# Same tile shapes in the RWKV chain, whole-width squares, and all PSUM banks in the last stage

## The chip, the core and the metric

The kernel runs on one core of one Trainium2 chip. The metric is the device time of one execution in microseconds (us). Before the change three runs took 1882.31, 1886.06 and 1886.7 us; the median is 1886.06.

## The reference, cut to what matters

One layer of a hybrid decoder for 1024 prompt tokens and 8 sample tokens that share all weights, in float32 (width 1024):

```python
h = rmsnorm(x, ln1); P = h @ w_in              # RWKV-7 | S5 | two merge gates
# RWKV-7, 8 heads of 64, for every token t:
sa = S @ (-kk_t)
S = S * w_t + outer(sa, kk_t * a_t) + outer(v_t, k_t)
y_t = S @ r_t                                  # then group norm, bonus, gate, w_rw_out
x += (sigmoid(g_rw) * rw + sigmoid(g_s5) * s5) @ w_out
x += ConvFFN(rmsnorm(x, ln2))                  # up 1024 -> 2 x 2816, causal conv, GELU gate, down
x += sigmoid(rmsnorm(x, ln3) @ w_ple_gate) * (p @ w_ple)
return rmsnorm(x, final_g), states
```

Each rmsnorm divides by the root of the mean square over the 1024 channels. Channels lie on partitions here (8 tiles of 128), so the sum over channels is a matmul with a matrix of ones over the tiles' summed squares.

## The kernel before, in words

Activations are stored transposed: 8 channel tiles of 128 partitions, tokens along the columns. Every float32 product with a large weight is split into two rounded parts ("hi" and "lo", fp32r), and each weight tile takes three matmuls, hi x hi, hi x lo and lo x hi. ScalarE (ACT) rounds the weight ("whi"), GpSimd (POOL) subtracts ("wlo"), and TensorE (PE) accumulates in a PSUM bank ("psm"). Plain float32 matmuls appear as two records each in the trace.

Stages: (1) the norm and the input projection in three blocks of 344 columns; (2) the S5 branch; (3) the RWKV recurrence, cut into chunks of 64 tokens, for 4 pairs of heads in two halves of 512 tokens, 8 units of 8 chunks; (4) the rest of the layer, in two "parts": columns 0 to 511 in one block of 512, and columns 512 to 1031 in two blocks of 260. Part 2 ends with the last stage (ple gate, final norm).

`chain` is the serial piece of stage 3. For chunk c with the state `So` it issues on PE: "S,AR" (`pp`, the state against the decayed keys, written to partitions 64 to 127), the two "Gm,UV" of the chunk before (`inner`, the part of the output inside a chunk, one per head, each to its half of the partitions), after a DVE addition (`pe`) the two "pe,Gm" (`up`, solving for the updates, one per head, to partitions 0 to 63), after a DVE copy (`UV`) "UV,BT" (`su`, the state's increment) and "AR,S" (the output from the old state). DVE then writes the new state `Sn`. The 64 x 64 heads make these matmuls differ in the rows and columns of the PE array that they use: a page row "128*64" is a matmul over 128 rows and 64 columns. Because other work is independent of the chain, projections ("psm") stand between its steps on PE.

The order on each engine is not written by hand. `Sched` records every operation with its dependencies and a priority, keeps an estimated cost per operation (and `SWITCH`, 90 ns, for a PE shape other than the one before), and repeatedly issues the operation that can start first on its modelled clock, by priority among those that could start then. A tile of a pool is handed out in the order in which the tiles of its tag were recorded. A change to one operation thus deals the order of all engines anew.

In `parts`, `sumsq` squares a tile on ACT into a buffer `sqt` (two of them, each claimed by a small memset on POOL) and adds it to `ssq`, on POOL for m up to 2 and on DVE above; `rstd` multiplies by ones on PE ("pstt"), and takes Ln and Exp on ACT into `rst`. In the last stage each tile m needs for each block a bank for the gate (`psg`) and one for `p @ w_ple` (`psp`). Part 2 has five banks of its own (`pm2`), while three (`pm`) of the eight are left from part 1. The last loop multiplies the 8 tiles by `rst`, tiles 3, 5 and 7 on POOL and the others on DVE, and stores them in pairs.

Of the kernel before, what the change touches and what calls it, by code (L numbers as in the profile page):

```python
# [9 lines left out]
F32 = mybir.dt.float32  # L10
F32R = mybir.dt.float32r
AF = mybir.ActivationFunctionType
# [5 lines left out]
P = 128  # L18
# [10 lines left out]
HW = 512  # L29
# [400 lines left out]
def build(tc, I, O, dbg=None):  # L430
# [106 lines left out]
    hs = ExitStack()  # L537
# [215 lines left out]

    def parts(ap, t0, n, blk, nmid, groups, pm, *nw):

# [57 lines left out]
        def sumsq(m, sl):  # L813
            if m == 0:
                G.tensor_tensor(ssq[:, sl], x2[m][:, sl], x2[m][:, sl], op=MUL)
            else:
                tmp = ta_("sqt", blk)
                S.activation(tmp, x2[m][:, sl], AF.Square)
                (V if m > 2 else G).tensor_tensor(ssq[:, sl], ssq[:, sl], tmp, op=ADD)

        def rstd(part=blocks):
            with g.prio(HI):
                for sl in part:
                    ps = pm.tile([P, blk], F32, name="pstt", tag="psm")
                    T.matmul(ps, ones, ssq[:, sl], start=True, stop=True)
                    S.activation(rst[:, sl], ps, AF.Ln, bias=epst[:, 0:1])
                sl = slice(part[0].start, part[-1].stop)
                S.activation(rst[:, sl], rst[:, sl], AF.Exp, scale=-0.5)
# [34 lines left out]
        with g.prio(HI):  # L863
            for m in range(8):
                hx.append(part(x2[m], "act", 8, pc("ln2", m)))
                with g.prio(HI + 1):
                    for sl in blocks:
                        sumsq(m, sl)

# [40 lines left out]
        with g.prio(HI):  # L910
            for k in range(2):
                pr = cv_()
                dma(pr, I["p"][k][:, tk])
                px.append(part(pr, "mid", nmid))
            for m in range(8):
                hx3.append(part(x2[m], "act", 8, pc("ln3", m)))
                with g.prio(HI + 1):
                    for sl in blocks:
                        sumsq(m, sl)
        for m in range(8):  # L920
            wg, wl = wtiles(I["w_ple_gate"][m], 8), wtiles(I["w_ple"][m], 2)
            pss = []
            for sl in blocks:
                with g.prio(MAIN):
                    psg = pm.tile([P, blk], F32, name="psm", tag="psm")
                    mmblk(psg, wg, hx3, sl.start, blk)
                    if m == 0 and len(blocks) == 1:
                        rstd()
                    psp = pm.tile([P, blk], F32, name="psm", tag="psm")
                    mmblk(psp, wl, px, sl.start, blk)  # L930
                    pss.append((psg, psp))
            if m == 0 and len(blocks) > 1:
                rstd()
            for sl, (psg, psp) in zip(blocks, pss):
# [8 lines left out]
        with g.prio(HI):  # L943
            if not shared:
                g.table("natural_log_exp_and_others", 6, rst[:, 0:1], tanh)
            for sl in blocks:
                rstd([sl])
                for m in range(8):
                    (G if m in (3, 5, 7) else V).tensor_tensor(x2[m][:, sl], x2[m][:, sl],
                                                               rst[:, sl], op=MUL)  # L950
                    if m % 2:
                        dma(O["y"][m - 1:m + 1, :, t0 + sl.start:t0 + sl.stop]
                            .rearrange("m p t -> p m t"), x2p[m // 2][:, :, sl])

    c2 = ExitStack()
    cvs = cp.tile([P, NH, 2], F32, name="cvs")
    parts(hp, 0, HW, HW, 4, (3, 2, 2, 3, 3, 3, 3, 3), pm, 2, 3)
    g.until_pools("rp", "p1", "pb", "pch", "py")
# [6 lines left out]
    parts(pool(c2, "pb_"), HW, NT - HW, (NT - HW) // 2, 5, (4, 3, 4, 4, 4, 3),  # L965
          pm2, 3, 5)
    g.drain()
# [308 lines left out]
def build_rwkv(g, rp, pb, pch, py, I, O, Pd, Wd, Ad, Yd, sg, ssh, omu, pc, pcs, dscr, dap, dma,  # L1276
# [35 lines left out]
    def headsum(ps, x, hi, bufs, lo):  # L1312
# [12 lines left out]
        T.matmul(ps, bor, lo, start=False, stop=True)  # L1325

    St = {}
    for k, j in ((0, 0), (1, 0), (2, 0), (3, 0), (0, 1), (1, 1)):
# [158 lines left out]
    def chain(p, hf, a, b):  # L1487
        AR, WC, Gm, BT, UV = a["AR"], a["WC"], b["Gm"], b["BT"], b["UV"]
        Y = py.tile([P, NC, CH], F32, name="Yps", tag="Y")
        ch = pch.tile([P, 3, P], F32, name="chp", tag="ch")  # L1490
        pp, up, su = ch[64:128, 0], ch[0:64, 1], ch[:, 2]
        heads = [slice(64 * h, 64 * h + 64) for h in range(2)]
# [8 lines left out]
        for c in range(NC):  # L1501
            n = hf * NC + c
            So, Sn = St[p, n % 2], St[p, (n + 1) % 2]
            first = n == 0

            if not first:
                T.matmul(pp, AR[:, c, 0], So, start=True, stop=True)
            if c:
                inner(c - 1, done, n == 1)
            pe = rp.tile([64, P], F32, name="pe", tag="pe", bufs=2)  # L1510
            gv = Gm[64:128, c, :, 0:64]
            if first:
                V.tensor_copy(pe.rearrange("p (h t) -> p h t", t=64), gv)
            else:
                h2 = lambda z: z.rearrange("p (h t) -> p h t", t=64)
                V.tensor_tensor(h2(pe), h2(pp), gv, op=ADD)
            for h, hs in enumerate(heads):
                T.matmul(up[:, hs], Gm[0:64, c, h, 0:64], pe[:, hs], start=h == 0, stop=h == 1)
            got = V.tensor_copy(UV[0:64, c], up)
# [227 lines left out]
```

## Time and profile before

| | us |
|---|---|
| median of three runs | 1886.06 |
| the profiled execution itself | 1882.29 |
| its span, first to last instruction | 1880.5 |
| PE busy in the span | 1815.4 |
| DVE busy | 1157.0 |
| ACT busy | 808.6 |
| POOL busy | 746.0 |

The span leaves out 1.8 us of the execution that lie around the first and the last instruction. A busy PE means that some matmul is in flight; matmuls overlap, so the distance between the starts of two of them, not a record's length, tells what one costs. The profile also gives the clock that was granted to PE, as a share of 2.4 GHz: 0.982 on average here.

### The profile page before, as it was taken

To read this page: it belongs to the slowest core of one execution; us is meant where nothing else is said; L and a number is where in the kernel's file an instruction comes from. 1 tells how busy PE (TensorE), PEld (TensorE's weight loads), DVE (VectorE), ACT (ScalarE), POOL (GpSimd) and SP (SyncE) were. 2 spreads that over 40 slices of the span, in tenths; PEclk is the share of its full clock that TensorE was granted. 3 is DMA by queue.
4 is the path that set the end of the run, shared out by engine and by line. 5 is a ranking of instruction groups with operands and counts; after the bars stand their busy time and mean duration, and the time that the engine had idled before them with its cause. 6 is when DMAs were issued, how large, how long until landed. Compare 5 with 4: busy or idle time off the path is not lost.

```text
span 1880.5 us, 32435 instructions
## 1 busy us (share of the span) xinstructions
PE 1815.4 (97%) x11946; PEld 1619.4 (86%) x11946; DVE 1157.0 (62%) x2386; ACT 808.6 (43%) x1455; POOL 746.0 (40%) x1089
## 2 busy tenths in 40 slices
PE   7999999999999999999999999999999999999987
PEld 6988888888889898986788888888889999999986
DVE  8899358767776786766555434446645444445565
ACT  4242444356543656444533333334554233333454
POOL 0000022124332433345555554455665444444453
PEclk9998999899999999999999999999999999999988
DMA  5534864323322254346343332233323233333322
GB/s 199 155 110 156 252 204 134 90 65 100 98 80 94 82 195 125 114 148 223 133 141 102 96 94 89 94 100 90 101 93 115 85 93 95 94 93 93 94 68 86
DMA packets 157950, 219.80 MB, mean 117 GB/s; under 512 B 48209, under 2 KB 81489, under 8 KB 157649
## 3 DMA queue, kind: packets, MB, share of 16 engines
q1 hardware_dynamic: 157792, 217.74, 36.9%
q8 instruction: 94, 1.54, 0.3%
q14 instruction: 64, 0.52, 0.1%
HBM read 174.94 MB, written 42.92 MB: 116 GB/s over the span
## 4 chain that ended last, share of the span: by engine, by line
PE 49%; DVE 4%; DMA 3%; POOL 2%; ACT 2%; issue 1%; SPq 0%; DVEq 0%; POOLq 0%; ACTq 0%
PE psm L417 47%; POOL wlo L417 1%; DVE x L417 1%; DVE cv L417 1%; PE chp L417 1%; DVE act L417 1%; DMA wraw<-in_w_out 1%; DMA wraw<-in_w_ffn_in 1%; DMA wraw<-in_w_ffn_out 0%; DMA wraw<-in_w_rw_out 0%; DMA wraw<-in_w_ple_gate 0%; ACT whi L417 0%; DMA gr<-gd 0%; DMA x<-in_x 0%; DVE mid L417 0%
## 5 line engine op out<-in xcount | busy, mean ns | idle before, releaser
L417 POOL TENSOR_TENSOR wlo<-wraw,whi 128x512 fp32r<-128x512 f32 (+2 forms) x432 | 550.4, 1281 | 475.2 <-ACT whi L417 428.5
L417 PE MATMUL psm<-act,whi 128*128 128x260 f32 (+1 forms) x2880 | 655.7, 322 | 3.9 <-ACT whi L417 2.2
L417 PEld LDWEIGHTS psm<-act,whi 128*128 128x128 f32 x2880 | 482.6, 189 | 53.3 <-ACT whi L417 4.1
L417 ACT ACTIVATE whi<-wraw 128x512 fp32r<-128x512 f32 (+2 forms) x468 | 275.0, 596 | 438.1 <-PE psm L417 269.4
L417 PE MATMUL psm<-act,wlo 128*128 128x260 f32 (+1 forms) x1440 | 461.8, 323 | 1.2 <-POOL wlo L417 1.1
L417 PE MATMUL psm<-mid,whi 128*128 128x260 f32 (+1 forms) x1344 | 307.5, 321 | 3.6 <-DVE cv L417 2.7
L417 PEld LDWEIGHTS psm<-act,wlo 128*128 128x128 f32 x1440 | 272.1, 189 | 26.6 <-POOL wlo L417 3.4
L417 PE MATMUL psm<-h1h,whi 128*128 128x344 f32 x816 | 273.6, 336 | 11.9 <-DVE h1h L417 11.9
L417 PE MATMUL psm<-h1l,whi 128*128 128x344 f32 x816 | 274.3, 336 | 0.1
L417 PE MATMUL psm<-h1h,wlo 128*128 128x344 f32 x816 | 271.8, 334 | 2.1 <-DVE wlo L417 2.1
L417 PEld LDWEIGHTS psm<-mid,whi 128*128 128x128 f32 x1344 | 222.8, 189 | 21.9 <-DVE cv L417 3.0
L417 PE MATMUL psm<-mid,wlo 128*128 128x260 f32 (+1 forms) x672 | 213.6, 322 | 0.2 <-POOL wlo L417 0.2
L417 PEld LDWEIGHTS psm<-h1h,whi 128*128 128x128 f32 x816 | 158.4, 194 | 16.4 <-issue 13.4
L417 DVE TENSOR_TENSOR x<-psm,x 128x260 f32<-128x260 f32 (+1 forms) x160 | 84.7, 531 | 133.8 <-PE psm L417 133.7
L417 PEld LDWEIGHTS psm<-h1h,wlo 128*128 128x128 f32 x816 | 158.5, 194 | 5.8 <-DVE wlo L417 2.4
L417 PEld LDWEIGHTS psm<-h1l,whi 128*128 128x128 f32 x816 | 158.5, 194 | 4.6 <-issue 1.1
L417 PEld LDWEIGHTS psm<-mid,wlo 128*128 128x128 f32 x672 | 126.7, 189 | 10.7 <-POOL wlo L417 0.6
L417 DVE TENSOR_TENSOR ta<-psm,rs 128x260 f32<-128x260 f32 (+1 forms) x66 | 34.0, 516 | 141.5 <-PE psm L417 132.9
L417 DVE SCALAR_TENSOR_TENSOR cv<-ta,par,cv 128x512 f32<-128x512 f32 x88 | 94.7, 1076 | 37.5 <-ACT cv L417 36.0
L417 DVE TENSOR_TENSOR mid<-cv,mid 128x260 fp32r<-128x260 f32 (+1 forms) x84 | 66.3, 795 | 26.4 <-ACT mid L417 25.6
L417 ACT ACTIVATE sw<-S,WC 64x64 f32<-64x64 f32 x120 | 41.1, 344 | 69.7 <-DVE S L417 67.8
L417 ACT ACTIVATE mid<-cv 128x260 fp32r<-128x260 f32 (+1 forms) x84 | 40.2, 487 | 59.4 <-DVE cv L417 54.0
(345 smaller groups left out, 2560.4 us busy)
## 6 DMA issues: line engine op xcount, KB each, us to landing
wraw<-in_w_ffn_in SPq DMA_DIRECT2D x176, 256.0 KB, 2.6
wraw<-in_w_in SPq DMA_DIRECT2D x68, 256.0 KB, 3.4
wraw<-in_w_ffn_out SPq DMA_DIRECT2D x64, 192.0 KB, 2.4
gd<-gt SPq DMA_DIRECT2D x16, 516.0 KB, 2.9
wraw<-in_w_out SPq DMA_DIRECT2D x32, 256.0 KB, 2.7
wraw<-in_w_ple_gate SPq DMA_DIRECT2D x32, 256.0 KB, 2.6
wraw<-in_w_ffn_out SPq DMA_DIRECT2D x32, 256.0 KB, 3.0
pd<-pt SPq DMA_DIRECT2D x12, 516.0 KB, 3.6
```

Of the source, the lines that this page charges most:

```text
L417: o.fn(*o.args, **o.kw)
```

## The change

1. In `chain`, "S,AR" takes both halves of `AR` as its weights and fills all 128 output partitions, of which the lower 64 are used. `pe` becomes one of two fixed tiles of 128 partitions, the upper 64 zeroed once, and "pe,Gm" contracts over all 128. The "Gm,UV" of the chunk before are recorded behind "pe,Gm" and wait for the DVE addition into `pe`, where they waited for the last chunk's state.
2. In `parts`, the squares for the second and third norm are taken over all columns of a part, in part 2 one of 520 where two of 260 were taken. (For the final norm they stay by block.)
3. `parts` is given a second pool of banks, `other`: for part 1 the same `pm`, for part 2 the three banks of part 1. In the last stage odd tiles use it for all but the first gate block, and the two "pstt" of the third norm lie in it.
4. The final norm of part 2 writes its factors twice: by one Exp to PSUM (`psr`), which DVE's products read, and by a second Exp to SBUF for POOL's.

```diff
-    def parts(ap, t0, n, blk, nmid, groups, pm, *nw):
+    def parts(ap, t0, n, blk, nmid, groups, pm, other, *nw):
...
-                tmp = ta_("sqt", blk)
+                tmp = ta_("sqt", sl.stop - sl.start)
...
-        def rstd(part=blocks):
+        def rstd(part=blocks, bank=None):
...
-                    ps = pm.tile([P, blk], F32, name="pstt", tag="psm")
+                    ps = (bank or pm).tile([P, blk], F32, name="pstt", tag="psm")
...
-                    for sl in blocks:
-                        sumsq(m, sl)
+                    sumsq(m, slice(0, n))
...
             pss = []
+            banks = [pm, other if m % 2 else pm]
             for sl in blocks:
+                if sl.start:
+                    banks[0] = banks[1]
                 with g.prio(MAIN):
-                    psg = pm.tile([P, blk], F32, name="psm", tag="psm")
+                    psg = banks[0].tile([P, blk], F32, name="psm", tag="psm")
...
-                    psp = pm.tile([P, blk], F32, name="psm", tag="psm")
+                    psp = banks[1].tile([P, blk], F32, name="psm", tag="psm")
...
-                rstd()
+                rstd(bank=other)
...
-                rstd([sl])
+                if shared:
+                    rstd([sl])
+                    rv = rst[:, sl]
+                else:
+                    ps = pm.tile([P, blk], F32, name="pstt", tag="psm")
+                    T.matmul(ps, ones, ssq[:, sl], start=True, stop=True)
+                    S.activation(rst[:, sl], ps, AF.Ln, bias=epst[:, 0:1])
+                    rv = other.tile([P, blk], F32, name="psr", tag="psm")
+                    S.activation(rv, rst[:, sl], AF.Exp, scale=-0.5)
+                    S.activation(rst[:, sl], rst[:, sl], AF.Exp, scale=-0.5)
                 for m in range(8):
-                    (G if m in (3, 5, 7) else V).tensor_tensor(x2[m][:, sl], x2[m][:, sl],
-                                                               rst[:, sl], op=MUL)
+                    if m in (3, 5, 7):
+                        G.tensor_tensor(x2[m][:, sl], x2[m][:, sl], rst[:, sl], op=MUL)
+                    else:
+                        V.tensor_tensor(x2[m][:, sl], x2[m][:, sl], rv, op=MUL)
...
+    rhs = []
+    for k in range(2):
+        t = rp.tile([P, P], F32, name=f"pe{k}")
+        G.memset(t[64:128], 0.0)
+        rhs.append(t)
...
-        pp, up, su = ch[64:128, 0], ch[0:64, 1], ch[:, 2]
+        pp, up, su = ch[:, 0], ch[0:64, 1], ch[:, 2]
...
             if not first:
-                T.matmul(pp, AR[:, c, 0], So, start=True, stop=True)
-            if c:
-                inner(c - 1, done, n == 1)
-            pe = rp.tile([64, P], F32, name="pe", tag="pe", bufs=2)
+                T.matmul(pp, AR[:, c].rearrange("p a b -> p (a b)"), So, start=True, stop=True)
+            pe = rhs[n % 2]
...
-                V.tensor_tensor(h2(pe), h2(pp), gv, op=ADD)
+                got = V.tensor_tensor(h2(pe[0:64]), h2(pp[0:64]), gv, op=ADD)
             for h, hs in enumerate(heads):
-                T.matmul(up[:, hs], Gm[0:64, c, h, 0:64], pe[:, hs], start=h == 0, stop=h == 1)
+                T.matmul(up[:, hs], Gm[:, c, h, 0:64], pe[:, hs], start=h == 0, stop=h == 1)
+            if c:
+                inner(c - 1, got, n == 1)
```

What this does to the order of the engines is shown at three places. First PE in the chain, one chunk between projections of 344 columns, before (a row gives output, operands and the output's size, "x2" that it stands twice):

```order
L417 MATMUL chp<-S_2733,AR 64x128
L417 MATMUL Yps<-Gm,UV 64x64 x2
L417 MATMUL psm<-h1h,whi 128x344
L417 MATMUL psm<-h1l,whi 128x344
L417 MATMUL psm<-h1h,wlo 128x344
L417 MATMUL chp<-pe,Gm 64x64 x2
...
L417 MATMUL chp<-UV,BT 128x128
L417 MATMUL Yps<-AR,S_2733 128x64
```

The same chunk of the changed kernel:

```order
L417 MATMUL chp<-S_2735,AR 128x128
L417 MATMUL psm<-h1h,whi 128x344
L417 MATMUL psm<-h1l,whi 128x344
L417 MATMUL psm<-h1h,wlo 128x344
...
L417 MATMUL chp<-pe_2730,Gm 64x64 x2
L417 MATMUL Yps<-Gm,UV 64x64 x2
...
L417 MATMUL chp<-UV,BT 128x128
L417 MATMUL Yps<-AR,S_2735 128x64
```

"S,AR" stands alone now and has the full size, and the two "Gm,UV" have moved behind the two "pe,Gm".

Second PE at the turn into the last stage, with buffer numbers, before: psm_11047 is the last bank of tile 0, psm_11061 the first of tile 1, the two pstt are the sums of the third norm.

```order
L417 MATMUL psm_11047<-mid_11012,wlo_11043 128x260
L417 MATMUL pstt_11048<-rs_10221,ones_66 128x260
L417 MATMUL pstt_11049<-rs_10221,ones_66 128x260
L417 MATMUL psm_11061<-act_11013,whi_11053 128x260 x2
L417 MATMUL psm_11061<-act_11013,wlo_11054 128x260
```

The same place now, where psm_11027 is the last bank of tile 0 and psm_11041 the first of tile 1:

```order
L417 MATMUL psm_11027<-mid_10999,wlo_11023 128x260
L417 MATMUL psm_11041<-act_11000,whi_11033 128x260 x2
L417 MATMUL psm_11041<-act_11000,wlo_11034 128x260
...
L417 MATMUL psm_11041<-act_11011,whi_11036 128x260 x2
L417 MATMUL pstt_11028<-rs_10215,ones_66 128x260
L417 MATMUL pstt_11029<-rs_10215,ones_66 128x260
L417 MATMUL psm_11041<-act_11011,wlo_11037 128x260
```

20 of the 24 matmuls of tile 1's first bank stand ahead of the two pstt now; none did.

Third POOL at the same place, from the split of tile 1's gate weights on, before (wlo is the split of a weight, 512 wide for a gate and 256 for the second product; sqt is the buffer of a square, tg one of the last stage):

```order
L417 TENSOR_TENSOR wlo<-wraw,whi 128x512 x2
L417 MEMSET sqt 128x2 x3
L417 TENSOR_TENSOR wlo<-wraw,whi 128x256
L417 MEMSET sqt 128x2 x2
L417 TENSOR_TENSOR wlo<-wraw,whi 128x512 x2
L417 MEMSET sqt 128x2 x3
L417 MEMSET tg 128x2 x2
```

And now:

```order
L417 TENSOR_TENSOR wlo<-wraw,whi 128x512 x2
L417 MEMSET sqt 128x2 x2
L417 TENSOR_TENSOR wlo<-wraw,whi 128x256
L417 MEMSET sqt 128x2
L417 TENSOR_TENSOR wlo<-wraw,whi 128x512
L417 MEMSET tg 128x2
```

Eight claims of a square's buffer stood there and three of them behind the splits of tile 2's gate weights; three stand there now, all ahead of those splits.

## Rows read from the trace of the kernel before

**Rows 1.** The page's totals: busy us, share of the span, instructions.

```profile
PE 1815.4 (97%) x11946; PEld 1619.4 (86%) x11946; DVE 1157.0 (62%) x2386; ACT 808.6 (43%) x1455; POOL 746.0 (40%) x1089
```

**Rows 2.** Stretches: length, busy us per engine, PE clock, DMA share, GB/s.

```profile
338.50:827.50 489.00, 480.26 (x3654) 418.19 (x3654) 356.85 (x950) 252.32 (x466) 165.50 (x289) 1.00 0.33 101
827.50:1018.40 190.90, 184.90 (x856) 148.06 (x854) 116.31 (x160) 81.12 (x148) 104.77 (x140) 0.98 0.50 166
1796.20:1812.50 16.30, 10.42 (x66) 8.33 (x65) 9.92 (x19) 8.94 (x20) 7.17 (x15) 0.85 0.25 81
1866.00:1880.50 14.50, 0.71 (x2) 0.30 (x2) 7.99 (x13) 3.49 (x7) 5.35 (x6) 0.60 0.43 147
...
1807.50:1817.80 10.30, 7.76 (x28) 6.29 (x29) 3.83 (x9) 6.42 (x11) 1.61 (x7) 0.50 0.12 42
```

**Rows 3.** Timeline of PE over one chunk: start, length, instruction, rows*columns, count.

```profile
570.90 0.32 PE L417 MATMUL psm<-h1l,whi 128*128 128x344 f32 x1
571.06 0.38 PE L417 MATMUL chp<-UV,BT 128*128 128x128 f32 x2
...
571.66 0.32 PE L417 MATMUL psm<-h1h,whi 128*128 128x344 f32 x1
...
572.14 0.32 PE L417 MATMUL psm<-h1h,whi 128*128 128x344 f32 x1
572.39 0.32 PE L417 MATMUL chp<-S,AR 128*64 128x128 f32 x1
...
573.13 0.32 PE L417 MATMUL psm<-h1h,wlo 128*128 128x344 f32 x1
573.29 0.32 PE L417 MATMUL psm<-h1h,whi 128*128 128x344 f32 x1
573.54 0.44 PE L417 MATMUL chp<-pe,Gm 64*64 64x64 f32 x4
...
574.17 0.32 PE L417 MATMUL psm<-h1h,wlo 128*128 128x344 f32 x1
...
574.96 0.32 PE L417 MATMUL psm<-h1l,whi 128*128 128x344 f32 x1
```

**Rows 4.** Timeline of PE where the two "Gm,UV" stand alone.

```profile
472.12 0.31 PE L417 MATMUL psm<-h1h,wlo 128*128 128x344 f32 x1
472.36 0.34 PE L417 MATMUL Yps<-Gm,UV 128*64 128x64 f32 x4
...
472.88 0.32 PE L417 MATMUL psm<-h1l,whi 128*128 128x344 f32 x1
```

**Rows 5.** Timeline of PE at the turn into the last stage.

```profile
1804.26 0.28 PE L417 MATMUL psm<-mid,wlo 128*128 128x260 f32 x1
1808.64 1.23 PE L417 MATMUL pstt<-rs,ones 128*128 128x260 f32 x2 [4.10 <-DVE rs L417]
1810.70 1.23 PE L417 MATMUL pstt<-rs,ones 128*128 128x260 f32 x2 [0.83 <-ACT rs L417]
1812.51 0.80 PE L417 MATMUL psm<-act,whi 128*128 128x260 f32 x2 [0.57 <-ACT rs L417]
```

**Rows 6.** Timeline of POOL and ACT there; in brackets the idle time before and its end.

```profile
1804.63 2.67 POOL L417 TENSOR_TENSOR wlo<-wraw,whi 128x512 fp32r<-128x512 f32 x2 [0.65 <-PE psm L417]
...
1807.37 0.73 ACT L417 ACTIVATE sqt<-x 128x260 f32<-128x260 f32 x2 [2.00 <-POOL sqt L417]
```

**Rows 7.** The last products by tile x: min/median/max ns, first and last start.

```profile
L417 DVE TENSOR_TENSOR x<-x,rs x10: 414/950/959, 1868.6 to 1874.9; 128x260 f32<-128x260 f32 x10
...
L417 POOL TENSOR_TENSOR x<-x,rs x6: 912/912/972, 1868.7 to 1873.1; 128x260 f32<-128x260 f32 x6
```

**Rows 8.** Groups by shape: count, busy us, mean ns of one, idle before.

```profile
L417 DVE TENSOR_TENSOR x<-psm,x 128x260 f32<-128x260 f32 x96 | 40.7, 426 | 65.4 <-PE psm L417 65.3
...
L417 POOL TENSOR_TENSOR rs<-rs,sqt 128x260 f32<-128x260 f32 x12 | 10.1, 846 | 1.5 <-ACT sqt L417 1.5
...
L417 ACT ACTIVATE rs<-rs 128x260 f32<-128x260 f32 x2 | 0.8, 412 | 0.0
```

More of the change, by code (lines that the diff above doesn't have):

```diff
@@ L917, in parts @@
                 with g.prio(HI + 1):
-                    for sl in blocks:
-                        sumsq(m, sl)
+                    sumsq(m, slice(0, n))
         for m in range(8):
@@ L956, in build @@
     cvs = cp.tile([P, NH, 2], F32, name="cvs")
-    parts(hp, 0, HW, HW, 4, (3, 2, 2, 3, 3, 3, 3, 3), pm, 2, 3)
+    parts(hp, 0, HW, HW, 4, (3, 2, 2, 3, 3, 3, 3, 3), pm, pm, 2, 3)
     g.until_pools("rp", "p1", "pb", "pch", "py")
@@ L965, in build @@
     parts(pool(c2, "pb_"), HW, NT - HW, (NT - HW) // 2, 5, (4, 3, 4, 4, 4, 3),
-          pm2, 3, 5)
+          pm2, pm, 3, 5)
     g.drain()
@@ L1506, in chain @@
             if not first:
-                T.matmul(pp, AR[:, c, 0], So, start=True, stop=True)
-            if c:
-                inner(c - 1, done, n == 1)
-            pe = rp.tile([64, P], F32, name="pe", tag="pe", bufs=2)
+                T.matmul(pp, AR[:, c].rearrange("p a b -> p (a b)"), So, start=True, stop=True)
+            pe = rhs[n % 2]
             gv = Gm[64:128, c, :, 0:64]
             if first:
-                V.tensor_copy(pe.rearrange("p (h t) -> p h t", t=64), gv)
+                got = V.tensor_copy(pe[0:64].rearrange("p (h t) -> p h t", t=64), gv)
             else:
                 h2 = lambda z: z.rearrange("p (h t) -> p h t", t=64)
-                V.tensor_tensor(h2(pe), h2(pp), gv, op=ADD)
+                got = V.tensor_tensor(h2(pe[0:64]), h2(pp[0:64]), gv, op=ADD)
             for h, hs in enumerate(heads):
-                T.matmul(up[:, hs], Gm[0:64, c, h, 0:64], pe[:, hs], start=h == 0, stop=h == 1)
+                T.matmul(up[:, hs], Gm[:, c, h, 0:64], pe[:, hs], start=h == 0, stop=h == 1)
+            if c:
+                inner(c - 1, got, n == 1)
             got = V.tensor_copy(UV[0:64, c], up)
```

## The prediction

> **What bounds the kernel now.** I read the engine totals first: TensorE (PE) is busy for 97% of the span and the next engine, DVE, for 62% [rows 1]. A change to this kernel therefore pays where it shortens matmul time itself or one of the few stretches in which PE waits. The table by stage says which those are [rows 2]. In the RWKV stretch (338.5 to 827.5) PE is busy 480.26 of 489 us. From 827.5 to 1018.4 it is idle for 6.0 us. At the turn into the last stage (1796.2 to 1812.5) it is idle 5.9 of 16.3 us, and the clock there is not full. After 1866 PE has nothing left to do and the rest of the span, 14.5 us, is a plain tail. The change touches the first, the third and the last of these.
>
> **Part 1, the chain.** I took the timeline of PE over one chunk while projections fill it [rows 3]. Fill matmuls of 344 columns follow each other every 0.158 us (574.17 to 574.96 is five steps). A group of chain matmuls costs what two fill matmuls around it are further apart than 0.316 us. For "UV,BT" with "AR,S" that is 571.66 - 570.90 - 0.316 = 0.444 us. For "S,AR" with the two "Gm,UV" it is 573.13 - 572.14 - 0.316 = 0.674 us, for the two "pe,Gm" 574.17 - 573.29 - 0.316 = 0.564 us. One chunk costs 1.682 us of PE. The last two have a price the first lacks: the matmul ahead of them and theirs stand 0.25 us apart (572.14 to 572.39, 573.29 to 573.54), the full-array group only 0.16 (570.90 to 571.06). So entering another tile shape costs 0.09 us, and leaving it costs again.
>
> After the change "S,AR" runs over the whole array, "pe,Gm" over 128 rows and 64 columns, and the two "Gm,UV", moved behind it, have the shape of "pe,Gm". Two shape borders per chunk go. Where two "Gm,UV" stand alone they cost 472.88 - 472.12 - 0.316 = 0.444 us [rows 4], 0.12 less than the two "pe,Gm" of equal column count; they write the two column halves and run side by side, while both "pe,Gm" write the lower half. So a 64-column matmul costs 0.12 us alone and nothing beside another half. Hence:
> - "S,AR" alone: the full-array pair less one 64-column matmul, 0.444 - 0.12 = 0.324 us.
> - "pe,Gm" with "Gm,UV": 0.564 + 0.12 = 0.684 us if the upper half runs beside the lower, 0.804 us if not. The trace has no such group; I take 0.684, since both are in one shape as in rows 4.
> - the third group as it is, 0.444 us.
>
> That is 1.452 us (or 1.572): 0.23 us saved per chunk (or 0.11). There are 8 units of 8 chunks, 60 of them with a state to multiply: 13.8 us if each stood apart. Not all do; some adjoin narrow preparation matmuls where a border is paid anyway. Counted over both PE orders the shape changes fall from 438 to 344; 94 fewer, two per chunk at 0.23 us, is 10.8 us. I take 10.8, with 5.2 (47 at 0.11) and 13.8 as ends. PE has no idle time to absorb it and part 1 of the next stage is fill enough, so it counts in full. "Gm,UV" now waits for the sum that feeds "pe,Gm"; the "pe,Gm" ahead of it in PE's queue waits for the same sum, so the fill and the "UV,BT" behind it wait no longer than they do now.
>
> The Trainium skill, "TensorEngine Tiling", section "Performance Considerations", would keep a contraction of 64 on a row tile for up to twice the throughput, which speaks against filling "pe,Gm" up with 64 rows of zeros; section "Tiling Modes" says that tiles of one mode work independently, while a change of mode drains the array. The rows side with the second: 128-row and 64-row matmuls of 64 columns differ only by the half they write. By the first alone the chain would keep next to nothing of its gain.
>
> **Part 2, the turn into the last stage.** PE finishes tile 0 of the gate matmuls at 1804.26 + 0.12 = 1804.38 and starts tile 1 at 1812.51: 8.1 us without stage matmuls [rows 5]. It waits 4.10 us for the sum of squares ("rs"), then the second "pstt" waits for ACT to empty the first one's bank (1808.64 to 1810.70), then tile 1 for the bank of the second. The clock over 1807.5 to 1817.8 is 0.50, so 1812.51 to 1817.8 runs at 1.2 instead of 2.4 GHz: half of 5.3, 2.65 us more [rows 2].
>
> After the change the two "pstt" and most of tile 1 use three idle banks. The order puts 20 matmuls of tile 1 ahead of "pstt"; one of 260 columns costs 0.158 x 260/344 = 0.12 us, so PE works on until 1804.38 + 2.4 = 1806.8. When are the squares summed? Before, ACT waited 2.00 us for a buffer whose memset stood behind two weight splits of 2.67 us on POOL [rows 6]. With whole-width squares there are 7 instead of 14 and the memset of the last stands ahead of that pair, so the sum should come 2.0 us sooner, at 1806.6. Then "pstt" starts at 1806.8, the pair takes about 1.2 us at full clock (1.23 each at half), neither waits for ACT, and ten more matmuls fit before tile 1 needs a bank that ACT empties. PE loses about 1.2 of the 8.1 us, and without the long idle stretch the clock stays up: 6.9 + 2.65 = 9.5; I take 9.0. At the low end the sum comes as late as now: the 20 matmuls and ten more are done early (3.6 us) and tile 1 goes on about 1.8 us sooner, 5.4 us and nothing for the clock. The squares of the earlier norm lie beside fill matmuls, so I cost their change at nothing; without that cover the pairs of 0.73 us on ACT [rows 6] would only become shorter.
>
> **Part 3, the tail.** The last norm multiplies 16 pieces: ten on DVE take 6.7 us (1868.6 to 1874.9 plus 0.41), 0.95 each while POOL multiplies and 0.41 after it; six on POOL take 0.91 each [rows 7]. A DVE product of the same size with one operand in PSUM takes 0.426 us on average over 96 [rows 8], so ten cost 4.3 us. POOL starts one Exp (0.41 us) later and takes 0.846 each as in its other sums, or, as I estimate, 0.75 undisturbed (those 0.846 are a mean over disturbed ones too): 0.41 + 6 x 0.75 = 4.9 us. That is now the later one: gain 6.7 - 4.9 = 1.8 us; ends 0.8 (POOL at 0.91: 0.41 + 5.5) and 2.4 (DVE last). The Trainium skill, "SBUF — State Buffer", section "Who interferes with whom", calls the port pair of DVE and GpSimd an exclusive lock, taken by a DVE operation with two SBUF inputs; by it POOL is free too and 1.8 holds, without it 0.8.
>
> **Sum.** 10.8 + 9.0 + 1.8 = 21.6 us off the profiled execution, which took 1882.29 us (span 1880.5): 1860.7. The median of the runs, 1886.06, lies 3.8 above that execution, so I predict 1864.5 us. Ends: 11.4 (5.2 + 5.4 + 0.8) and 25.7 us. Every engine's order is dealt anew, which moves small waits; as a scale I take the 6.0 us idle between 827.5 and 1018.4, either way.
>
> **Rivals.**
> - The two halves don't overlap or the padded matmul costs more: the chain brings 5.2, sum 16.0, 1870 us. For it: no row shows this group. Against: rows 4.
> - The sum of squares is as late as now: 5.4 in part 2 and no clock, sum 18.0, 1868 us. For it: weight splits still stand in POOL's queue.
> - The borders were not the cost, or the new order gives it all back in small waits: 1883 to 1886 us. Against: the same 0.09 us at each border.
> - Slower: the chain now ends later against the fill; its last chunks stand behind the last gated-unit matmul among part 1's output projection. Part 2's first 192 matmuls (192 x 0.12 = 23 us), which fill PE while part 1 passes its second norm, need the chain's very last product. If that comes after part 1's w_out is through, this fill falls out of the hole, and at half clock for some us after: 23 + 3 = 26 against 21.6, about 1890 us. For it: 6.0 us idle there already. Against: counted along both PE orders, that fill begins only some 6 us of matmuls later than now.
>
> **How the numbers follow.** Forecast 0.57, the four rivals 0.15, 0.12, 0.09, 0.07. A measurement tells about 0.3%, 5.7 us, from no change. Faster than 1880.4: forecast and first two, 0.84; same 0.09; slower 0.07. The range goes from 25.7 + 6 off the median, rounded in to 1855, up to 1877, past both smaller gains with half of the 6 us and more.
>
> **What would show it.** In the new profile: the steps 0.25 us before "S,AR" gone, and "pe,Gm" with "Gm,UV" as one group of about 0.68 us; the chain's end not followed by a hole before 1018; "pstt" twice in a row without a wait for ACT, PE idle under 2 us there and no 0.50 clock behind it; ten last products of 0.43 us on DVE. I am wrong if the group costs 0.8 or more, if "pstt" still waits for "rs" for 4 us, or if idle time between 827 and 1018 grows past 15 us.

## The result and the profile after

The changed kernel took 1857.3 us (median of four runs, 1855.01 to 1876.07; the profiled one 1858.5). Against runs of the kernel before on the same chip (median 1884.18) the ratio is 0.9878, with a 95% interval from 0.9836 to 0.9919. Six more runs in a later session gave 0.9866 (0.9828 to 0.9903). The forecast was 1864.5 us, in a range from 1855 to 1877.

One thing has to be known to read all the numbers below. Runs of one and the same kernel scatter by more than most of these edits bring, and the mean clock listed with each run explains most of it: through 77 runs of the kernel before (clock 0.971 to 0.987, three sessions on three chips) goes a line of 1.51 us per 0.001 of mean clock; the scatter is 5.3 us around their mean and 2.1 us around that line. So each experiment has two numbers here: the ratio with its interval, and the difference to the kernel before **at a mean clock of 0.980**, worked out with that line from its runs, with two standard errors. Three runs that count as slow are left out of both (one each of the kernel before, of "Gm,UV" early and of the order only). For the changed kernel (ten runs) the second number is -22.2 ± 0.9 us. What an edit gains by keeping the clock up is nearly all taken out of the second number and is in the first. With a line through the runs of its own session alone, a kernel's number moves by up to 1.3 us; the four single parts come from one session, the pieces of the chain from a second, the versions without narrow shapes and the squares by block from a third.

Totals of the page after, to hold against [rows 1]: PE is busy for 16.4 us less, and the span is 23.8 us shorter.

```profile
span 1856.7 us, 32382 instructions
...
PE 1799.0 (97%) x11946; PEld 1616.2 (87%) x11946; DVE 1135.5 (61%) x2376; ACT 810.6 (44%) x1445; POOL 738.7 (40%) x1071
```

The same stretches as in [rows 2], cut at the same events (first chain matmul, last gated-unit matmul, first matmul of part 2's second norm, the turn, the last stage's end):

```profile
335.40:822.00 486.60, 472.83 (x3622) 420.39 (x3621) 346.66 (x941) 253.97 (x466) 164.40 (x292) 0.98 0.34 103
822.00:1013.00 191.00, 187.83 (x918) 152.72 (x918) 121.45 (x171) 82.69 (x153) 110.08 (x143) 1.00 0.52 168
1786.00:1797.00 11.00, 10.49 (x84) 10.16 (x83) 7.92 (x12) 6.53 (x11) 5.94 (x10) 1.00 0.33 103
1843.50:1856.70 13.20, 1.11 (x6) 0.49 (x4) 4.95 (x14) 4.76 (x10) 4.19 (x6) 0.70 0.48 161
```

The first row is the surprise: the RWKV stretch is hardly shorter (486.6 against 489 us) though the chain got cheaper. Idle time there is 486.60 - 472.83 = 13.8 us, where it was 8.7, and the clock is 0.98, where it was 1.00 (rounded). In the second row idle time is down from 6.0 to 3.2 us; at the turn it is 0.5 of 11 us, at full clock. Between the starts of the same PE instructions the two profiled executions differ by -3.1 us up to the chain, -2.3 in the chain's stretch, -3.0 and -3.5 up to the end of part 1, -4.0 up to the turn, -5.7 in the last stage and -2.1 in the tail: 23.7 together. The -3.1 is not the change's: the kernel before and the three single parts below that leave the chain alone start the chain anywhere between 334.7 and 338.5 us.

PE over one chunk after, to hold against [rows 3] (start, length, instruction, rows*columns of the array, count):

```profile
616.79 0.31 PE L417 MATMUL psm<-h1l,whi 128*128 128x344 f32 x1
617.03 0.39 PE L417 MATMUL chp<-pe,Gm 128*64 128x64 f32 x3
617.20 0.27 PE L417 MATMUL Yps<-Gm,UV 128*64 128x64 f32 x1
617.25 0.22 PE L417 MATMUL chp<-pe,Gm 128*64 128x64 f32 x1
617.31 0.28 PE L417 MATMUL Yps<-Gm,UV 128*64 128x64 f32 x3
617.52 0.43 PE L417 MATMUL psm<-h1h,wlo 128*128 128x344 f32 x1
617.79 0.32 PE L417 MATMUL psm<-h1h,whi 128*128 128x344 f32 x1
617.95 0.32 PE L417 MATMUL psm<-h1l,whi 128*128 128x344 f32 x1
618.10 0.38 PE L417 MATMUL chp<-UV,BT 128*128 128x128 f32 x2
...
618.70 0.31 PE L417 MATMUL psm<-h1h,whi 128*128 128x344 f32 x1
...
619.17 0.32 PE L417 MATMUL psm<-h1h,whi 128*128 128x344 f32 x1
619.33 0.40 PE L417 MATMUL chp<-S,AR 128*128 128x128 f32 x2
619.49 0.40 PE L417 MATMUL psm<-h1l,whi 128*128 128x344 f32 x1
619.73 0.32 PE L417 MATMUL psm<-h1h,wlo 128*128 128x344 f32 x1
```

By the prediction's measure (distance of the fill matmuls around a group, less 0.316), "pe,Gm" with "Gm,UV" costs 617.79 - 616.79 - 0.316 = 0.68 us, "UV,BT" with "AR,S" 0.43, "S,AR" 0.24. "Gm,UV" begins between the passes of "pe,Gm": the two column halves do run side by side. "S,AR" starts 0.16 us after the fill matmul ahead of it, without the 0.25 of before, and the fill behind it starts 0.16 us after its first pass.

PE at the turn after (idle time in brackets where there is any), to hold against [rows 5]:

```profile
1791.77 0.28 PE L417 MATMUL psm<-mid,wlo 128*128 128x260 f32 x1
1791.89 0.40 PE L417 MATMUL psm<-act,whi 128*128 128x260 f32 x2
...
1794.06 0.40 PE L417 MATMUL psm<-act,whi 128*128 128x260 f32 x2
1794.30 1.04 PE L417 MATMUL pstt<-rs,ones 128*128 128x260 f32 x4
1794.98 0.47 PE L417 MATMUL psm<-act,wlo 128*128 128x260 f32 x1
```

Tile 1 runs from 1791.89 on, both "pstt" (two passes each) follow each other at 1794.30, and tile 1 goes on 0.68 us later.

The tail by tile x after (min/median/max ns, first and last start), to hold against [rows 7]; the stores to y last:

```profile
L417 DVE TENSOR_TENSOR x<-x,psr x10: 418/419/425, 1847.0 to 1850.0; 128x260 f32<-128x260 f32 x10
L417 SPq DMA_DIRECT2D out_y<-x x8: 372/452/682, 1847.8 to 1852.2; - x8
L417 POOL TENSOR_TENSOR x<-x,rs x6: 731/732/735, 1847.5 to 1850.9; 128x260 f32<-128x260 f32 x6
```

### The profile page after: what moved, and what is told of

It reads as the page before. It is cut to its first block, busy times and chain, and to the rows that moved or that the text cites. A ratio compares the mean times of both kernels' runs of the same rounds, so it can differ in the third digit from the quotient of the medians.

```text
span 1856.7 us, 32382 instructions
## 1 busy us (share of the span) xinstructions
PE 1799.0 (97%) x11946; PEld 1616.2 (87%) x11946; DVE 1135.5 (61%) x2376; ACT 810.6 (44%) x1445; POOL 738.7 (40%) x1071
## 4 chain that ended last, share of the span: by engine, by line
PE 71%; DVE 10%; DMA 4%; ACT 3%; issue 3%; POOL 2%; SPq 1%; POOLq 0%; DVEq 0%; ACTq 0%
PE psm L417 62%; PE chp L417 2%; PE gp L417 1%; DMA yf<-yq 1%; DVE Tm L417 1%; PE gvp L417 1%; DVE Tt L417 1%; PE Yps L417 1%; DMA raw<-pd 1%; SPq L417 1%; DVE m L417 1%; DVE cv L417 1%; POOL wlo L417 1%; DMA wraw<-in_w_rw_out 1%; DVE Xi L417 1%
## 5 line engine op out<-in xcount | busy, mean ns | idle before, releaser
L417 DVE SCALAR_TENSOR_TENSOR cv<-ta,par,cv 128x512 f32<-128x512 f32 x88 | 89.7, 1019 | 38.3 <-ACT cv L417 36.9
L417 ACT ACTIVATE cv<-cv 128x512 f32<-128x512 f32 (+1 forms) x44 | 28.0, 636 | 87.6 <-DVE cv L417 87.6
```

Of the source, the lines that this page charges most:

```text
L417: o.fn(*o.args, **o.kw)
```

## The experiments

**One part alone.** The theory was the prediction's: the shape borders pay for the chain's gain, the banks and the earlier sum for the turn's, PSUM operands for the tail's. Four kernels carry one part each on the kernel before.

The chain alone:

```diff
-        pp, up, su = ch[64:128, 0], ch[0:64, 1], ch[:, 2]
+        pp, up, su = ch[:, 0], ch[0:64, 1], ch[:, 2]
...
-                T.matmul(pp, AR[:, c, 0], So, start=True, stop=True)
-            if c:
-                inner(c - 1, done, n == 1)
-            pe = rp.tile([64, P], F32, name="pe", tag="pe", bufs=2)
+                T.matmul(pp, AR[:, c].rearrange("p a b -> p (a b)"), So, start=True, stop=True)
+            pe = rhs[n % 2]
...
-                T.matmul(up[:, hs], Gm[0:64, c, h, 0:64], pe[:, hs], start=h == 0, stop=h == 1)
+                T.matmul(up[:, hs], Gm[:, c, h, 0:64], pe[:, hs], start=h == 0, stop=h == 1)
+            if c:
+                inner(c - 1, got, n == 1)
```

> Only the chain's edit, on the kernel before; shape changes on PE fall from 438 to 344. My theory (each shape border costs, and PE has no idle time there): about 11 us less than before (8 to 14), the end of part 1's last third-norm product about 12 us earlier, the chain's groups as in the whole change (0.69 and about 0.24 us). Rival (the borders are free, the gain of the whole change is the dealt order or the last stage): within 3 us of before.

Ratio 0.9906 (0.9888 to 0.9924); at 0.980 -15.1 ± 1.0 us. The rival is out; 11 us were too few, and 15.1 lies above the 14 of the expectation. In its profile the idle time of [rows 2] between 827.5 and 1018.4 is gone too:

```profile
827.50:1018.40 190.90, 189.16 (x909) 154.09 (x909) 119.02 (x164) 83.22 (x153) 111.56 (x142) 1.00 0.50 161
```

1.7 us idle at full clock, against 6.0 us at 0.98 before. (These are the same times and not the same events; from the last gated-unit matmul to part 1's next "pstt" it is 1.7 against 5.1 us.)

The banks alone:

```diff
+            banks = [pm, other if m % 2 else pm]
...
-                    psp = pm.tile([P, blk], F32, name="psm", tag="psm")
+                    psp = banks[1].tile([P, blk], F32, name="psm", tag="psm")
...
-                rstd()
+                rstd(bank=other)
```

> Only the other pool of banks in the last stage. My theory: the squares are as late as before, so the second sum waits for nothing but the squares and tile 1 goes on 5.4 us sooner (4 to 7) at the turn; PE still idles 2 to 4 us there. Rival (the squares alone set the turn, the banks bring nothing without them): 0 to 2 us less.

Ratio 0.9957 (0.9936 to 0.9979), -3.8 ± 1.4 us at 0.980 and so, with the clock that is kept at the turn, about 8 us by the ratio. PE does all 24 matmuls of tile 1's first bank, runs dry, waits 1.29 us for the sum, and both "pstt" follow without a wait for ACT:

```profile
1817.40 0.28 PE L417 MATMUL psm<-act,wlo 128*128 128x260 f32 x1
1818.97 1.44 PE L417 MATMUL pstt<-rs,ones 128*128 128x260 f32 x4 [1.29 <-DVE rs L417]
```

From part 1's last "pstt" to PE's last instruction it takes 423.8 us, the kernel before 430.7: 6.9 less, with 5.4 (4 to 7) expected. The rival is out.

The squares alone:

```diff
-                    for sl in blocks:
-                        sumsq(m, sl)
+                    sumsq(m, slice(0, n))
```

> Only the squares over all columns, for the second and the third norm. My theory: at the turn the sum of squares is ready 2 us sooner, so 2 us less (0 to 4); the second sum of the norm still waits for ACT to empty the first one's bank, 1 us or more, and the clock still falls to half there. Rival (the squares are the turn's whole cost): 6 us less or more, and the clock stays up.

Ratio 0.9989 (0.9969 to 1.0010), -1.7 ± 1.3 us at 0.980. The wait for the sum is 2.02 us instead of 4.10: 2.1 us sooner, as expected. The second "pstt" still waits for ACT, and behind it the clock falls to 0.50 for 6.8 us (10.2 before).

```profile
1819.56 0.84 PE L417 MATMUL pstt<-rs,ones 128*128 128x260 f32 x2 [2.02 <-DVE rs L417]
1820.97 1.24 PE L417 MATMUL pstt<-rs,ones 128*128 128x260 f32 x2 [0.57 <-ACT rs L417]
1822.78 0.80 PE L417 MATMUL psm<-act,whi 128*128 128x260 f32 x2 [0.57 <-ACT rs L417]
```

The last norm's factors alone:

```diff
+                    rv = other.tile([P, blk], F32, name="psr", tag="psm")
+                    S.activation(rv, rst[:, sl], AF.Exp, scale=-0.5)
...
-                                                               rst[:, sl], op=MUL)
+                        V.tensor_tensor(x2[m][:, sl], x2[m][:, sl], rv, op=MUL)
```

> Only the last norm's factors also in PSUM. My theory: ten products on DVE at 0.42 us each and the six on POOL at 0.73, the stretch from the last matmul to the end 1.8 to 2.1 us shorter, which five rounds can hardly tell from nothing; the profile's tail shows it. Rival (the second Exp delays POOL by as much as it gains): tail as long as before within 0.5 us, 12.1 us from the last matmul to the end of the span.

Ratio 0.9993 (0.9970 to 1.0015), -1.2 ± 1.0 us at 0.980: nothing by the ratio, as expected. In the profile the tail is 10.2 us instead of 12.1, DVE's products take 416 ns and POOL's 740. At 0.980 the four parts add up to -21.8 us and the whole change to -22.2: within some 2.5 us, the errors of the five numbers together, they don't help or hinder each other.

**The squares once more, taken out of the change.** The same edit undone in the changed kernel:

> The changed kernel with the squares of the second and third norm by block again, 14 of 260 columns in place of 7 of 520 at the turn. Theory: the sum comes 2 us later, PE runs out of gate matmuls about 1.5 us before it as with the banks alone, then the two sums follow each other without a wait for ACT; 2 to 3 us more than the changed kernel. Rival (with the banks in place the squares are hidden anyway): no idle time ahead of the sum, no difference.

Ratio 0.9894 (0.9855 to 0.9933), -19.0 ± 1.1 us at 0.980, 3.2 less than the whole change. "pstt" waits 1.28 us for the sum, as with the banks alone, then no more:

```profile
1813.35 1.44 PE L417 MATMUL pstt<-rs,ones 128*128 128x260 f32 x4 [1.28 <-DVE rs L417]
```

So of the turn's two causes neither edit takes both away: the banks give PE work and the "pstt" their place, the squares bring the sum in time for that work.

**The chain in pieces.** What in the chain pays: no border, wider matmuls, or the order? Three kernels take one piece out of the chain's edit, one has only the order. First "S,AR" narrow again (with `pp` on its old half):

```diff
-                T.matmul(pp, AR[:, c].rearrange("p a b -> p (a b)"), So, start=True, stop=True)
+                T.matmul(pp, AR[:, c, 0], So, start=True, stop=True)
```

> The chain's edit alone, but with S,AR over 64 columns as before, so that it stands alone in a shape of its own; shape changes on PE 444, against 344 with the whole chain edit and 438 before. Theory (borders between shapes cost): S,AR alone 0.35 us instead of 0.24, its first matmul 0.09 us later behind the fill; 5 us more than the whole chain edit by the groups (47 x 0.11), 11 us by counting changes at 0.115. Rival (a matmul over half the array is the cheaper one, the borders are free): S,AR alone 0.24 us or less, time as with the whole chain edit.

```profile
570.57 0.32 PE L417 MATMUL psm<-h1l,whi 128*128 128x344 f32 x1
570.82 0.43 PE L417 MATMUL chp<-S,AR 128*64 128x128 f32 x2
571.18 0.43 PE L417 MATMUL psm<-h1h,wlo 128*128 128x344 f32 x1
571.45 0.31 PE L417 MATMUL psm<-h1h,whi 128*128 128x344 f32 x1
```

Alone in its shape "S,AR" costs 571.45 - 570.57 - 0.316 = 0.56 us, over the whole array 0.24. The border ahead of it takes the expected 0.09 us (0.25 against 0.16), but the fill behind it starts 0.36 us after its start, against 0.16 for the wide one: its two passes and the way out take 0.20 more. From its last pass to the second fill matmul behind it the medians are 0.47 us narrow and 0.27 wide, so that leaving costs about 0.19 here. Where 64 columns move and not 128, it costs less: 0.42 us behind the narrow "pe,Gm" with "Gm,UV" and 0.33 behind the full-array "UV,BT" with "AR,S", so about 0.09. The ratio, 0.9914 (0.9886 to 0.9942), is that of the whole chain edit and would speak for the rival; but these six runs had a mean clock of 0.985. At 0.980 it is -8.2 ± 1.9 us, 6.9 less than the chain edit, and PE's work, from which the clock is taken out in another way, says the same (table below).

Then "pe,Gm" over 64 rows again:

```diff
-                T.matmul(up[:, hs], Gm[:, c, h, 0:64], pe[:, hs], start=h == 0, stop=h == 1)
+                T.matmul(up[:, hs], Gm[0:64, c, h, 0:64], pe[0:64, hs], start=h == 0, stop=h == 1)
```

> The chain's edit alone, but with pe,Gm over 64 rows as before, Gm,UV over 128 rows behind it; 395 shape changes. Theory: the group pe,Gm with Gm,UV costs 0.78 us (one border of 0.09 more than 0.69) to 0.90 us (the two halves of columns also no longer run side by side); 4 to 10 us more than the whole chain edit. Rival (64 rows of zeros are work that costs, borders are free): 0.69 us or less, time as with the whole chain edit or below it.

```profile
569.54 0.32 PE L417 MATMUL psm<-h1l,whi 128*128 128x344 f32 x1
569.79 0.44 PE L417 MATMUL chp<-pe,Gm 64*64 64x64 f32 x4
570.17 0.34 PE L417 MATMUL Yps<-Gm,UV 128*64 128x64 f32 x4
570.43 0.43 PE L417 MATMUL psm<-h1h,wlo 128*128 128x344 f32 x1
570.70 0.32 PE L417 MATMUL psm<-h1h,whi 128*128 128x344 f32 x1
```

The group costs 0.84 us (median 0.83), inside the expected 0.78 to 0.90: "Gm,UV" no longer begins until "pe,Gm" is through. Ratio 0.9917 (0.9891 to 0.9943), -11.4 ± 1.3 us at 0.980, 3.7 less than the chain edit, just under the 4 to 10 expected. So 64 rows of zeros are cheaper than a border. Keeping "pe,Gm" on 64 rows, as the Trainium skill would by the section that the prediction cited ("TensorEngine Tiling", "Performance Considerations"), lost here; two row tiles side by side, from which that section has its gain, no run tried. With the section "Tiling Modes", by which tiles of one mode work independently and a change of mode drains the array, the trace agrees: 0.69 us in one shape, 0.83 in two.

Then "Gm,UV" back behind "S,AR":

```diff
+            if c:
+                inner(c - 1, done, n == 1)
             pe = rhs[n % 2]
...
-            if c:
-                inner(c - 1, got, n == 1)
```

> The chain's edit alone, but with Gm,UV issued behind S,AR as before; 456 shape changes. Theory: S,AR with two Gm,UV 0.61 us (0.15 full array, border 0.09, 0.27, leaving 0.11), pe,Gm alone 0.57 us as before; a chunk 1.63 us against 1.38 with the whole edit and 1.69 before, so 12 us more than the whole chain edit and nearly as slow as before. Rival (the gain is in the wider S,AR or in the padding, the order adds nothing): half or more of the chain edit's gain stays, 8 us or more less than before.

Ratio 1.0009 (0.9975 to 1.0044), -2.8 ± 1.0 us at 0.980: nearly as slow as before, as expected. "S,AR" with "Gm,UV" costs 0.70 us (0.61 expected), "pe,Gm" alone 0.57. And the order without the shapes:

```diff
-            if c:
-                inner(c - 1, done, n == 1)
...
+            if c:
+                inner(c - 1, got, n == 1)
```

> Only the place of Gm,UV behind pe,Gm, on the kernel before, all shapes as before; 491 shape changes against 438. Counting changes at 0.115 us: 6 us slower than before. By the groups: S,AR alone 0.35 us, pe,Gm with Gm,UV 0.78 to 0.90 us, a chunk 1.58 to 1.70 us against 1.69, so 0 to 5 us less than before. Rival (order and waits are the gain, shapes are not): 10 us or more less than before.

Ratio 1.0008 (0.9981 to 1.0035), -1.1 ± 1.1 us at 0.980. The rival is out: order and waits alone bring nothing. The time lies in the range that I had reckoned by the groups, 0 to 5 us less, but by luck: "S,AR" alone cost 0.56 us where I had 0.35, and with that the groups would have made it slower (next).

Put together (medians in us over the groups that stand alone between fill matmuls; the third group is 0.45 everywhere; "times 47" is the chunk's difference to before by the count that the prediction used):

| kernel | with S,AR | with pe,Gm | chunk | times 47 | at 0.980 | PE's work | idle |
|---|---|---|---|---|---|---|---|
| before | 0.67 | 0.57 | 1.69 | 0 | 0 | 1787.9 | 53.4 |
| whole chain edit | 0.24 | 0.69 | 1.38 | -14.8 | -15.1 ± 1.0 | 1777.1 | 52.1 |
| pe,Gm over 64 rows | 0.24 | 0.83 | 1.52 | -8.0 | -11.4 ± 1.3 | 1783.4 | 51.8 |
| S,AR narrow | 0.56 | 0.69 | 1.69 | +0.2 | -8.2 ± 1.9 | 1787.2 | 45.9 |
| Gm,UV early | 0.70 | 0.57 | 1.72 | +1.2 | -2.8 ± 1.0 | 1788.9 | 49.6 |
| order only | 0.56 | 0.83 | 1.84 | +7.1 | -1.1 ± 1.1 | 1787.1 | 49.1 |

The two columns on the right are of one profiled execution each. "PE's work" is the time that PE is busy up to its last matmul, less half of what of it lies at half clock (1.2 GHz), so that executions at different clocks can be compared; the four kernels with the chain of before have 1787.2 to 1789.2 us of it. "Idle" is PE's idle time up to there.

Each piece undone costs time, and 6 to 12 us of PE's work against the whole edit. But all four mixed kernels are 3 to 8 us faster than their chunks say. With "S,AR" narrow and "Gm,UV" early the two columns tell why: PE has as much to do as the chunks say, and waits 7.5 and 3.8 us less than in the kernel before. With only the order changed the work does not grow by 7.1 us, and the whole chain edit spares 10.8 and not 14.8; so the count of 47 is the prediction's and not a fixed number of chunks. For these two and for "pe,Gm" over 64 rows work and idle time together miss the time at equal clock by 3 to 5 us, and not all to the same side. That is not settled.

**A version without any narrow shape.** If borders are the cost, the last narrow group should go too:

```diff
-        UV = rp.tile([P, NC, P], F32, name="UV", tag="UV", bufs=2)
+        uvn[0] += 1
+        UV = uvs[uvn[0] % 2]          # [P, NC, 3, CH], the middle third zero
...
-                then(op, Y[hs, c], UV[:, c, hs], Gm[:, c, h, 64:128], start=first, stop=True)
+                then(op, Y[:, c], UV[:, c, h:h + 2].rearrange("p a b -> p (a b)"),
+                     Gm[:, c, h, 64:128], start=first and h == 0, stop=h == 1)
...
-                T.matmul(up[:, hs], Gm[:, c, h, 0:64], pe[:, hs], start=h == 0, stop=h == 1)
+                T.matmul(up[:, hs], Gm[:, c, h], pe[:, hs], start=h == 0, stop=h == 1)
```

> The changed kernel with no narrow shape left in the chain: pe,Gm takes all 128 columns of Gm as weights (the upper half of the result unused), Gm,UV takes for each head the 64 columns of updates with 64 columns of zeros beside them and accumulates into all 128 rows (UV is laid out as updates, zeros, updates in two fixed tiles; Tm and its scratch have one buffer, av shares L's, to make room). 226 shape changes against 344. Theory (borders cost): the group is eight passes of about 0.058 us and 0.084 to the fill, 0.55 us instead of 0.69, 47 x 0.14 = 6.5 us less than the changed kernel; by counting changes, 118 at 0.126, 15 us less. Rival (the gain was the two column halves side by side, which this gives up): the group 0.69 us or more, time as the changed kernel or slower.

> The changed kernel once more, as the reference for the two versions beside it and for more runs at known clocks. Theory: about 1860 us, 22 us less than before at the same granted clock. Rival (its gain was the clock of the first few runs): 15 us or less at the same granted clock.

The changed kernel beside it took 1861.26 us, -22.5 ± 1.1 us at 0.980, as expected. The all-wide version has a ratio of 0.9934 (0.9905 to 0.9964) and -8.6 ± 1.0 us: some 14 us slower than the changed kernel, though it has 118 shape changes fewer. My theory fell here, and the time is what the rival said.

```profile
568.13 0.32 PE L417 MATMUL psm<-h1h,whi 128*128 128x344 f32 x1
568.29 0.55 PE L417 MATMUL chp<-pe,Gm 128*128 128x64 f32 x4
568.68 0.61 PE L417 MATMUL Yps<-Gm,uv 128*128 128x64 f32 x4
569.10 0.40 PE L417 MATMUL psm<-h1l,whi 128*128 128x344 f32 x1
569.34 0.32 PE L417 MATMUL psm<-h1h,wlo 128*128 128x344 f32 x1
```

No border at 568.29, but the group costs 569.34 - 568.13 - 0.316 = 0.89 us (median 0.92, so 47 x 0.23 = 11 us). PE's work is 1792.3 us, against 1774.9 in the changed kernel, so the loss is in the matmuls and not in waits for the buffers that were given up. After a first step of 0.055 us its passes start 0.111 us apart, where those of "pe,Gm" in the changed kernel start 0.058 us apart from the second on. Eight passes 0.058 us apart, one behind the other, would have made a group of some 0.57 us (0.16 to enter, 7 x 0.058, 0.33 to the second fill matmul, less 0.316); so giving up the two halves side by side, the rival's reason, is not what made it dear. The weight loads differ. In the all-wide version (min/median/max ns):

```profile
L417 PEld LDWEIGHTS chp<-pe,Gm x256: 186/191/286, 333.7 to 811.8; 128*128 128x128 f32 x128
```

in the changed kernel, and last in the kernel before, with half the rows:

```profile
L417 PEld LDWEIGHTS chp<-pe,Gm x256: 132/138/231, 335.4 to 827.1; 128*64 128x64 f32 x128
```

```profile
L417 PEld LDWEIGHTS chp<-pe,Gm x256: 129/135/223, 338.5 to 821.3; 64*64 64x64 f32 x128
```

A load of 128 columns is 0.05 us longer than one of 64, and so is the step between passes. I read it so that a pass of 64 moving columns is too short to hide the longer load. The Trainium skill ("TensorE: Matmul & The Clock Gate", section "LDWEIGHTS (loading the stationary operand)") says that a load's time goes by its columns and not by its rows. The trace agrees: 138 and 135 ns with 128 and 64 rows, 191 ns with twice the columns, and steps of 0.058 and 0.111 us. In "pe,Gm" 64 more rows cost nothing and 64 more columns did; "S,AR", where 128 columns move in each pass, took 64 more columns without harm.

The same version with one product of the tail moved from POOL to DVE:

```diff
-                    if m in (3, 5, 7):
+                    if m in ((3, 5, 7) if shared or not sl.start else (5, 7)):
```

> The version with no narrow shape in the chain, and tile 3 of the last block's products on DVE instead of POOL (DVE 11 products of 0.42 us, POOL 5 of 0.73). Theory: last product and end of the span 0.5 to 0.7 us earlier after the last matmul (9.4 us instead of 10.0), else as the version beside it; five rounds can't tell that from nothing. Rival (the store or DVE ends last already): 10.0 us as in the changed kernel.

Ratio 0.9916 (0.9884 to 0.9948), -8.8 ± 1.0 us at 0.980. The tail is 10.1 us, against 10.0 in the changed kernel; the rival was right. POOL and the stores of that version:

```profile
1862.11 3.50 POOL L417 TENSOR_TENSOR x<-x,rs 128x260 f32<-128x260 f32 x5 [5.38 <-ACT rs L417]
```

```profile
1862.40 5.02 SPq L417 DMA_DIRECT2D out_y<-x  x8
```

POOL is through 0.7 us sooner (3.50 us instead of 4.19), but the eight stores stand one behind the other on SP's queue for 5.02 us, 5.03 in the changed kernel. Now they set the end. No version beat the changed kernel.

## Why the prediction came out right

**The chain** (10.8 us; 15.1 measured at equal clock). The mechanism and the new group were right: 0.684 us forecast, 0.689 the median. The step that was mis-sized is "S,AR alone: the full-array pair less one 64-column matmul, 0.324 us". It measured 0.24 (median): what stands beside "UV,BT" in that pair costs 0.21 us and not the 0.12 that I had taken from the narrow groups. The all-wide version fits as a reason: "AR,S" too moves 64 columns over weights of 128, and two steps of 0.111 us make 0.22, two of 0.058 the 0.12. The 0.324 was 0.085 us too much for each chunk, 47 x 0.085 = 4.0 us. The prediction said that leaving a narrow shape costs and gave no size; the size, about 0.09 us in its groups, was already in their prices.

The count of 47 was somewhat high. Up to part 1's first "pstt" behind the chain the two orders do the same matmuls but for one, and from the chain's first matmul to there PE's work (as in the table) fell from 562.6 to 549.7 us in the two profiled executions, 12.9; over four profiles of each order the means differ by 12.6. At 0.31 us a chunk that is 41 chunks. Idle time over that stretch is the same in the means of four (14.7 and 14.6 us), so some 2.5 us of the 15.1 are not found there.

**"Every engine's order is dealt anew, which moves small waits."** It did, both ways: 5.0 us more idle time in the RWKV stretch, 2.8 less behind it (in the means of four profiles 3.2 more there and 3.3 less from there to the "pstt"). In the profiled execution the clock took more back: 20.5 us at half clock in the RWKV stretch, against 4.7 before, which is 7.9 us lost. That is this execution's, not the change's: with the order of before it is 4.7 to 41.5 us in four profiles.

**The chain's end** came later, as the slower rival said: its last product is at 831.2 us, behind the last gated-unit matmul at 822.0, where it was at 823.7 and ahead of it (827.4). No hole followed; idle time up to 1013 is 3.2 us. That part 2's fill begins hardly later was the right reading: its first matmul over 260 columns starts at 884.1, where it started at 883.5.

**The turn** (9.0 us). All three steps came as written: 20 matmuls of tile 1 ahead of "pstt", the sum in time, no wait for ACT, no half clock behind it. From part 1's last "pstt" to PE's last instruction the changed kernel takes 421.0 us, against 430.7: 9.7. The two "pstt" take 0.68 us (1794.30 to 1794.98) and not the 1.2 of the prediction, which is 0.5 of the 0.7 us. The second rival (the sum as late as now) is what the banks alone and the squares by block show: 1.3 us of waiting. Its price was too dark, though: with the banks alone 6.9 us came and not 5.4, and the clock stayed up there too.

**The tail** (1.8 us) is 12.1 - 10.0 = 2.1 us shorter. DVE's ten products take 3.4 us and not 4.3, since in a row each starts 0.34 us after the last; POOL's take 0.732 each, near the 0.75 estimated. POOL free beside DVE agrees with the lock that the Trainium skill describes ("SBUF — State Buffer", "Who interferes with whom"): 732 ns instead of 912 [rows 7]. But POOL isn't the later one, as the prediction had it: the stores are.

**The sum**, 21.6 us, looks better against -22.2 at equal clock than it is, and that is luck: 2.65 us of it are clock kept up at the turn, which a comparison at equal clock takes out. Without them 10.8 + 6.35 + 1.8 = 18.95 us stand against 15.1 + 5.5 + 1.2 = 21.8 for the single parts: the chain 4 us too small, the turn and the tail 1.5 too large together. With the clock in it, by the ratios, the change brought 23 and 25 us.

## What to carry to other kernels

Between matmuls of another shape a small matmul cost its own passes, about 0.09 us to enter its shape and 0.09 (64 moving columns) to 0.19 us (128) to leave it; so give neighbours one shape, pad the contraction with zero rows where that does it, and put the narrow ones into one group. Widen the weights' columns only where enough columns move to hide the longer load. Compare runs at the same granted clock before you believe a fraction of a per cent, and price a group by the distance of the matmuls around it in the trace, not by counting shape changes; even so, a group's price times a count missed the whole kernel's time by 3 to 8 us here when the edit also changed what waits.

## What was not expected of the hardware

- One order of instructions, two clocks: 495 to 590 us in the kernel before and in the kernel with only the squares changed, whose PE does the same matmuls in the same order up to 1035 us. The clock is the number behind POOL's count:

```profile
495.00:590.00 95.00, 94.68 (x777) 79.77 (x777) 70.23 (x207) 48.52 (x96) 27.34 (x48) 1.00 0.26 80
```

```profile
495.00:590.00 95.00, 95.00 (x661) 79.15 (x658) 55.84 (x152) 41.32 (x82) 24.73 (x43) 0.80 0.24 69
```

The first ran at 2.4 GHz throughout; the second had two pieces at 1.2 GHz, from 499.0 for 20.5 us and from 567.3 for 17.1. PE is busy but for 0.3 us in the first and throughout in the second, and does 116 matmuls fewer at 0.80. In the 29 us before the clock fell at 499.0 PE was never idle for more than 0.38 us. What decides it stays open.

- A matmul over half of the columns, alone between full-array matmuls, cost more than twice the full one (0.56 against 0.24 us for "S,AR").
- With operands in SBUF and PSUM, DVE's products of 260 columns took 0.42 us each and started 0.34 us apart, while POOL worked undisturbed at 0.73.
